# Feed-forward products: another order at the start of a block, wider h splits, residual updates spread

## The chip, the cores and the metric

One core of a Trainium2 chip runs the kernel. The metric is the device time of one execution in microseconds; three runs of the kernel before gave a median of 2126.9 (2126.14 to 2127.26).

## The reference, cut to what matters

The kernel computes one layer of a hybrid encoder for 512 rows of 2048 float32 values. A mixer (input projection, short convolution, gated linear attention) ends in an output projection with a residual. The change touches what comes behind it:

```python
    x = x + y @ w_out[l]
    h = rmsnorm(x, norm2_g[l])
    x = x + jnp.square(jax.nn.relu(h @ w_ff1[l])) @ w_ff2[l]
return rmsnorm(x, norm_f_g)
```

`w_ff1` is 2048 x 8192 and `w_ff2` 8192 x 2048. The change leaves what is computed as it is.

## The kernel before, in words

**Split products.** A float32 factor is held as two fp32r tiles: hi, a cast by ScalarE, and lo, the rest, subtracted by VectorE (`split_w`, lines 607 to 612, for weights). A product is three matmuls: hi by hi, hi by lo, lo by hi. So TensorE needs hi first, and lo two matmuls later at most.

**Seven products for eight.** Both feed-forward products are cut into 2 x 2 quarters, and seven products of sums of quarters (forms 1 to 7) replace eight. The weights' sums are w1 = b11 + b12 (form 5), w3 = w1 + b21 (form 6), w4 = w3 + b22 (form 4) and w7 = b11 + b21 (form 7), made by VectorE in `plus` (lines 614 to 617); forms 1, 3 and 2 are the raw quarters b12, b21, b22. Quarters come by SP's DMA queue into four raw buffers (`load_quarters`), and hi and lo have three buffers each, shared by all weights.

**The h forms.** While the output projection runs in column chunks 0 to 4 (`out_chunk`), `h_pair(p)` (lines 539 to 557) makes the forms of h for a pair of 128-column blocks: `h_block` transposes on TensorE and scales on VectorE, and `put_form` casts and subtracts one 128 x 256 form at a time. Pairs 0 to 6 are hooked into chunks 1, 2 and 4; pair 7 needs the last chunk and comes behind it, at line 580.

**First product, FF1** (lines 620 to 675). 32 steps g, each of seven products of 8 pairs x 3 = 24 matmuls of 128 x 256, in the order 1, 5, 7, 3, 6, 2, 4 (`product`). Results are combined, squared and, as forms for the second product, kept in DRAM (`a_keep`); the last two steps' results are kept whole in `a_last`.

**Second product, FF2** (lines 763 to 811). Four blocks of the inner dimension; in each, four column blocks n; in each n, two groups grp of seven products (`product2`), both in `ORDER` = 1, 6, 5, 3, 7, 2, 4. A product has 24 matmuls, in group 1 of the last block 12. `form(blk, grp, f)` (lines 689 to 706) brings one activation form from `a_keep` through a staging tile (four of them: two of tag st for even places in the order, two fixed slots of the h forms for odd places) and splits it; the first group's forms of the next block are made at n = 3 in group 1, the second group's at n = 0 in group 0. At the end of group 1, `evict` (lines 722 to 761) combines PSUM banks into four result tiles c, 128 x 512. In block 0 they are written to `c_keep`, in blocks 1 and 2 added to it by accumulating DMAs of the POOL queue, and in block 3 VectorE adds what `c_keep` holds (tile s, line 738) and updates the residual x with it (line 742, twice a tile).

**The end** (from line 837). The last 512 rows of `w_ff2` are multiplied in the plain way, tile e, and the final norm follows.

**What sets the order.** The program text gives every instruction a priority; when the kernel is built, a planner with times of its own puts each engine's instructions in a fixed order, the earliest of the text first among those that it holds ready. An instruction can so stand ahead of others that come earlier in the text. At run time each engine and queue takes its instructions in that fixed order and waits where one isn't ready.

Of the kernel before, what the change touches and what calls it, by code (L numbers as in the profile page):

```python
# [14 lines left out]
P = 128  # L15
# [24 lines left out]
def hymba_kernel(  # L40
# [444 lines left out]
    c_keep = [[tc.dram_tile([P, 2, HALF], F32, name=f"c_keep{n}{q}") for q in range(4)] for n in range(4)]  # L485
    hf = ctx.enter_context(tc.tile_pool(name="hf", bufs=1))
# [20 lines left out]
    def form_places(p):  # L507
        if p == 0:
            for n, f in enumerate(FORMS):
                wide_forms[f] = [  # L510
                    hf.tile([P, 4, HALF], F32R, name=f"S{q}{f}", tag=f"h{2 * n + m}") for m, q in enumerate("hl")
                ]
        if p < 4:
            for f in FORMS:
                hforms[p][f] = [t[:, p, :] for t in wide_forms[f]]
            return
        k = 2 * (p - 4)
        two = [
            [act.tile([P, 4, HALF], F32R, name=f"S{q}{p}{e}", tag=f"s{k + e + 8 * m}") for m, q in enumerate("hl")]
            for e in range(2)  # L520
        ]
        for n, f in enumerate(FORMS):
            hforms[p][f] = [t[:, n % 4, :] for t in two[n // 4]]

    def h_block(kt, pool):
        b = bank(f"htr_{kt}", "aux")
        n, k = divmod(kt, 4) if kt < 12 else divmod(kt - 6, 2)
        for i in range(NT):
            T.transpose(b[:, i * P : (i + 1) * P], xs[n][i][:, k * P : (k + 1) * P], ident)
        h = pool.tile([P, SEQ], F32, name=f"h_{kt}", tag=f"h{kt % 2}", bufs=1)  # L530
        V.scalar_tensor_tensor(out=h, in0=b, scalar=g2t[:, kt : kt + 1], in1=r1b, op0=ALU.mult, op1=ALU.mult)
        return h

    def put_form(p, f, src):
        hi, lo = hforms[p][f]
        S.copy(hi, src)
        V.tensor_tensor(out=lo, in0=src, in1=hi.bitcast(F32), op=ALU.subtract)

    def h_pair(p, pool):

        form_places(p)
        h1, h2 = (h_block(2 * p + e, pool) for e in range(2))
        a, b = slice(0, HALF), slice(HALF, SEQ)
        put_form(p, 1, h1[:, a])
        put_form(p, 2, h2[:, a])
        put_form(p, 4, h2[:, b])

        def minus(f, in0, in1):
            d = pool.tile([P, HALF], F32, name=f"d{f}_{p}", tag=f"d{f % 2}", bufs=2)
            V.tensor_tensor(out=d, in0=in0, in1=in1, op=ALU.subtract)  # L550
            put_form(p, f, d)
            return d

        d5 = minus(5, h1[:, b], h2[:, b])
        minus(7, h1[:, b], h1[:, a])
        d6 = minus(6, h1[:, a], d5)
        minus(3, h2[:, a], d6)

    with tc.tile_pool(name="n2", bufs=1) as n2:
# [36 lines left out]
    wt = ctx.enter_context(tc.tile_pool(name="wt", bufs=1, reuse_waits="tile"))  # L596

    def load_quarters(src, i0, n, name):

        raws = []  # L600
        for q in range(4):
            raw = wp.tile([P, UNIT], F32, name=f"raw_{name}{q}", tag="raw", bufs=RAWS)
            nc.sync.dma_start(raw[:, :n], src[i0 + q])
            raws.append(raw[:, :n])
        return raws

    def split_w(src, n, name):
        hi = wp.tile([P, UNIT], F32R, name=f"hi_{name}", tag="hi", bufs=3)
        lo = wp.tile([P, UNIT], F32R, name=f"lo_{name}", tag="lo", bufs=3)
        S.copy(hi[:, :n], src)  # L610
        V.tensor_tensor(out=lo[:, :n], in0=src, in1=hi[:, :n].bitcast(F32), op=ALU.subtract)  # L611
        return hi, lo

    def plus(in0, in1, n, name):
        w = wt.tile([P, 1024], F32, name=f"w_{name}", tag="w", bufs=3)
        V.tensor_tensor(out=w[:, :n], in0=in0, in1=in1, op=ALU.add)  # L616
        return w[:, :n]


    with tc.tile_pool(name="f1", bufs=1, reuse_waits="tile") as f1:  # L620
        for g in range(NPAIR):
            b12, b11, b21, b22 = load_quarters(w_ff1, 4 * g, 1024, f"f1_{g}")

            def product(f, w, dst, start):
                hi, lo = split_w(w, 1024, f"f1_{g}{f}")
                for p in range(8):
# [14 lines left out]
            product(1, b12, ba, True)  # L641
            q1 = half("q1")
            S.copy(q1, ba[:, :HALF])
            w1 = plus(b11, b12, 1024, f"f1_{g}5")
            product(5, w1, bc, True)
            q5 = half("q5")
            S.copy(q5, bc[:, :HALF])
            product(7, plus(b11, b21, 1024, f"f1_{g}7"), bd, True)
            product(3, b21, bc, False)
            w3 = plus(w1, b21, 1024, f"f1_{g}6")  # L650
            product(6, w3, bb, True)
# [35 lines left out]
    with tc.tile_pool(name="ff", bufs=1, reuse_waits="tile") as ff:  # L687
# [77 lines left out]
        for f in ORDER:  # L765
            form(0, 0, f)
        for blk in range(4):
            for n in range(4):
# [15 lines left out]
                for grp in range(2):  # L784
# [10 lines left out]
                    for f in ORDER:  # L795
# [10 lines left out]
                        if grp == 1:  # L806
                            evict(blk, n, f, dst, had)
# [154 lines left out]
```

## Time and profile before

| | us |
|---|---|
| median of 3 runs | 2126.9 |
| the profiled execution | 2126.53 |
| its span, first to last instruction | 2124.8 |
| TensorE busy | 2073.0 (98%) |
| VectorE busy | 1491.6 (70%) |
| ScalarE busy | 887.9 (42%) |
| POOL busy | 106.3 (5%) |
| FF1 begins / FF2 begins / last block of FF2 begins | about 786 / 1431 / 1916 |

The span lies inside the execution; 1.7 us lie around it. A matmul's listed duration (0.28 us) is longer than its share of the time, since matmuls overlap: what counts is the distance from one start to the next. The page's engines are PE (TensorE), PEld (its weight loads), DVE (VectorE), ACT (ScalarE), POOL (GpSimd) and SP (SyncE, a DMA queue here). A shape is partitions x elements.

### The profile page before, as it was taken

Reading aid. Unit: us, or ns where it says so; the run is one execution under the profiler, and the core shown is the slowest. Engines: PE = TensorE matmul, PEld = TensorE weight load, DVE = VectorE, ACT = ScalarE, POOL = GpSimd, SP = SyncE. Lnnn points to the kernel's source line nnn. Section 1 sums busy time; section 2 is a strip of 40 time slices with the busy share of each in tenths; the row PEclk is TensorE's granted clock in tenths of the full one; section 3 lists DMA queues with packets and bytes.
Section 4 is the critical chain, followed back from the end, with each engine's and each line's share of the span. In section 5 each row is a group of like instructions: output and inputs, shape, how many; then the busy total and the mean of one; then the engine's idle time right before and its main releaser. Section 6 shows DMA issues by size and latency. Waiting matters only on the chain.

```text
span 2124.8 us, 34341 instructions
## 1 busy us (share of the span) xinstructions
PE 2073.0 (98%) x14408; PEld 1925.0 (91%) x14408; DVE 1491.6 (70%) x1780; ACT 887.9 (42%) x1126; POOL 106.3 (5%) x161
## 2 busy tenths in 40 slices
PE   8999999999999999999999999999999999997987
PEld 7988878778788889999999999999999999997886
DVE  5232236756754468888888888888798798797786
ACT  6242213222233344554554554555354353353343
POOL 0000000000020000000000000000000001101000
PEclk9999999999999999999999999999999999999999
DMA  7223322222253324545445445457466476567342
GB/s 295 87 82 97 99 80 89 70 79 89 80 170 117 130 88 146 166 150 162 145 152 161 143 153 162 142 174 249 130 207 200 130 210 188 158 176 211 109 145 99
DMA packets 88314, 303.95 MB, mean 143 GB/s; under 512 B 10197, under 2 KB 10245, under 8 KB 87648
## 3 DMA queue, kind: packets, MB, share of 16 engines
q1 hardware_dynamic: 69120, 242.64, 35.9%
q0 software_dynamic: 19040, 59.13, 9.6%
q8 instruction: 112, 1.84, 0.4%
q14 instruction: 42, 0.34, 0.0%
HBM read 252.19 MB, written 49.55 MB: 142 GB/s over the span
## 4 chain that ended last, share of the span: by engine, by line
PE 91%; DVE 4%; DMA 2%; issue 1%; ACT 1%; ACTq 0%; DVEq 0%; POOLq 0%
PE f L717 23%; PE f1c L630 9%; PE f1a L630 8%; PE f1d L630 4%; PE f1e L630 4%; PE f1b L630 4%; PE tm_op L75 3%; PE tm_op L76 3%; PE tm_op L77 3%; PE fm_ch L75 2%; PE fm_cc L75 2%; PE tm_v L76 1%; PE tm_v L75 1%; PE tm_v L77 1%; PE fm_og L77 1%; PE fm_cb L76 1%
## 5 line engine op out<-in xcount | busy, mean ns | idle before, releaser
L717 PE MATMUL f<-lo_f,ah 128*128 128x256 f32 x1568 | 446.7, 285 | 20.2 <-DVE lo_f L611 20.2
L717 PE MATMUL f<-hi_f,ah 128*128 128x256 f32 x1568 | 443.3, 283 | 8.2 <-ACT ah L704 4.9
L717 PE MATMUL f<-hi_f,al 128*128 128x256 f32 x1568 | 443.9, 283 | 0.0
L610 ACT CAST hi_f<-w_f 128x1024 fp32r<-128x1024 f32 (+1 forms) x256 | 261.6, 1023 | 341.0 <-PE f L717 147.3
L611 DVE TENSOR_TENSOR lo_f<-w_f,hi_f 128x1024 fp32r<-128x1024 f32 (+1 forms) x256 | 303.9, 1189 | 120.6 <-ACT hi_f L610 119.3
L717 PEld LDWEIGHTS f<-lo_f,ah 128*128 128x128 f32 x1568 | 299.6, 191 | 21.9 <-DVE lo_f L611 21.8
L717 PEld LDWEIGHTS f<-hi_f,ah 128*128 128x128 f32 x1568 | 299.7, 191 | 8.6 <-ACT ah L704 5.1
L717 PEld LDWEIGHTS f<-hi_f,al 128*128 128x128 f32 x1568 | 300.0, 191 | 0.0
L610 ACT CAST hi_f<-raw_f 128x1024 fp32r<-128x1024 f32 (+1 forms) x192 | 196.5, 1024 | 198.1 <-PE f L717 82.9
L611 DVE TENSOR_TENSOR lo_f<-raw_f,hi_f 128x1024 fp32r<-128x1024 f32 (+1 forms) x192 | 227.4, 1184 | 3.6 <-ACT hi_f L610 3.6
L616 DVE TENSOR_TENSOR w_f<-raw_f,raw_f 128x1024 f32<-128x1024 f32 (+1 forms) x128 | 152.3, 1190 | 42.0 <-DMA raw_f<-in_w_ff 39.6
L616 DVE TENSOR_TENSOR w_f<-w_f,raw_f 128x1024 f32<-128x1024 f32 (+1 forms) x128 | 152.4, 1190 | 29.4 <-DMA raw_f<-in_w_ff 23.1
L630 PE MATMUL f1c<-Sh,hi_f 128*128 128x256 f32 x512 | 144.7, 283 | 3.2 <-ACT hi_f L610 3.2
L630 PE MATMUL f1c<-Sh,lo_f 128*128 128x256 f32 x512 | 144.7, 283 | 0.0
L630 PE MATMUL f1c<-Sl,hi_f 128*128 128x256 f32 x512 | 144.4, 282 | 0.0
L630 PE MATMUL f1a<-Sh,hi_f 128*128 128x256 f32 x512 | 144.2, 282 | 0.0
L630 PE MATMUL f1a<-Sh,lo_f 128*128 128x256 f32 x512 | 144.1, 282 | 0.0
L630 PE MATMUL f1a<-Sl,hi_f 128*128 128x256 f32 x512 | 144.0, 281 | 0.0
L75 PE MATMUL tm_op<-hi_op,yh 128*128 128x512 f32 (+1 forms) x304 | 106.2, 349 | 0.0
L76 PE MATMUL tm_op<-lo_op,yh 128*128 128x512 f32 (+1 forms) x304 | 105.3, 346 | 0.0
L77 PE MATMUL tm_op<-hi_op,yl 128*128 128x512 f32 (+1 forms) x304 | 105.0, 345 | 0.0
L630 PEld LDWEIGHTS f1c<-Sh,hi_f 128*128 128x128 f32 x512 | 97.4, 190 | 3.4 <-ACT hi_f L610 3.4
(359 smaller groups left out, 4846.3 us busy)
## 6 DMA issues: line engine op xcount, KB each, us to landing
raw_f<-in_w_ff SPq DMA_DIRECT2D x240, 512.0 KB, 3.8
a_keep<-y POOLq DMA_DIRECT2D x30, 896.0 KB, 5.1
st<-a_keep SPq DMA_DIRECT2D x49, 512.0 KB, 4.9
c_keep<-c POOLq DMA_DIRECT2D x48, 256.0 KB, 5.2
raw_op<-in_w_out SPq DMA_DIRECT2D x22, 512.0 KB, 3.6
raw_og<-in_w_feat SPq DMA_DIRECT2D x16, 512.0 KB, 3.6
raw_cc<-in_w_feat SPq DMA_DIRECT2D x16, 512.0 KB, 3.6
raw_ch<-in_w_feat SPq DMA_DIRECT2D x16, 512.0 KB, 3.7
```

The costliest lines, as they stand in the source:

```text
L75: T.matmul(dst, l[0], r[0], start=start, stop=False)
L76: T.matmul(dst, l[0], r[1], start=False, stop=False)
L77: T.matmul(dst, l[1], r[0], start=False, stop=stop)
L610: S.copy(hi[:, :n], src)
L611: V.tensor_tensor(out=lo[:, :n], in0=src, in1=hi[:, :n].bitcast(F32), op=ALU.subtract)
L616: V.tensor_tensor(out=w[:, :n], in0=in0, in1=in1, op=ALU.add)
L630: T.matmul(dst[:, :HALF], l[:, c], r, start=start and p == m == 0, stop=p == 7 and m == 2, skip_group_check=True,)
L717: T.matmul(d, l[:, k, t], r[:, c], start=grp == k == i == e == 0, stop=grp == 1 and k == m - 1 and e == 2, skip_group_check=True,)
```

## The change

- `load_quarters`, `split_w` and `plus` move up in the text; the pool `wt` is opened earlier, with two buffers for sums in place of three, and a pool `stage` takes over the two st tiles. `block_forms` makes a sum when its form is asked for, w3 and w4 in place of the sum that they start from.
- `h_pair` writes both transposed blocks into one tile of eight 256-wide places, makes the four differences in three operations, and from pair 4 on splits places 0 to 3 and 5 to 7 as two wide operations each.
- The first FF1 step: its weights are loaded ahead of `h_pair(7)` in the text, and forms 1, 5 and 7 are split there. Products 1, 5 and 7 run over pairs 0 to 6 first, and pair 7 follows.
- FF2: group 0 uses the order 1, 3, 2, 5, 7, 6, 4, group 1 the old one. `form` counts places by the group's own order; the loop that stages the second group's forms goes over group 0's order.
- Block 3: the rows of x come in 32 loads of 128 x 256, eight in each n behind group 0, where 8 loads of 128 x 1024 stood at n = 0. For n = 0 to 2 a result tile is added to s by an accumulating DMA of the POOL queue; for n = 3 VectorE adds it. The updates of x (`residual`) are put off: one tile's after each product of the next n's group 0, and those of n = 3 into the end, before the first update of columns 512 to 1023.

```diff
+    def block_forms(src, i0, n, name):
+        b12, b11, b21, b22 = load_quarters(src, i0, n, name)
+        w = {}
+        def parts_of(f):
+            if f in (5, 6) and 1 not in w:
+                w[1] = plus(b11, b12, n, f"{name}5")
+                w["early"] = f == 6
+            if f == 6:
+                w[3] = plus(w[1], b21, n, f"{name}6", None if w["early"] else w[1])
+            if f == 4:
+                w[4] = plus(w[3], b22, n, f"{name}4", w[3])
+            if f == 7:
+                w[7] = plus(b11, b21, n, f"{name}7")
+            v = {1: b12, 3: b21, 2: b22, 5: w.get(1), 6: w.get(3), 4: w.get(4), 7: w.get(7)}[f]
+            return split_w(v, n, f"{name}{f}")
+        return parts_of
...
+        V.tensor_tensor(
+            out=h[:, 0:2, :], in0=h[:, 4:5, :].to_broadcast([P, 2, HALF]), in1=h[:, 3:8:4, :], op=ALU.subtract
+        )
+        V.tensor_tensor(out=h[:, 5, :], in0=h[:, 3, :], in1=h[:, 1, :], op=ALU.subtract)
+        V.tensor_tensor(out=h[:, 2, :], in0=h[:, 6, :], in1=h[:, 5, :], op=ALU.subtract)
...
+        for e, (a, b) in enumerate(((0, 4), (5, 8))):
...
+            S.copy(hi[:, : b - a, :], h[:, a:b, :])
+            V.tensor_tensor(
+                out=lo[:, : b - a, :], in0=h[:, a:b, :], in1=hi[:, : b - a, :].bitcast(F32), op=ALU.subtract
+            )
...
+        first_forms = block_forms(w_ff1, 0, 1024, "f1_0")
+        ready = {f: first_forms(f) for f in (1, 5, 7)}
         h_pair(7, n2)
...
+            if g == 0:
+                for f, b in ((1, ba), (5, bc), (7, bd)):
+                    product(f, b, True, range(7))
+                product(5, bc, False, (7,))
+                product(1, ba, False, (7,))
+            else:
+                product(1, ba, True)
...
+                product(7, bd, False, (7,))
+            product(3, bc, False)
+            product(6, bb, True)
...
-    ORDER = (1, 6, 5, 3, 7, 2, 4)
+    ORDERS = ((1, 3, 2, 5, 7, 6, 4), (1, 6, 5, 3, 7, 2, 4))
...
+        def residual(n, q, c):
+            for i in range(2):
+                k = q // 2 * 2 + i
+                xc = x3t[k][q % 2][:, n, :]
+                V.scalar_tensor_tensor(
+                    out=xc, in0=c[:, i, :], scalar=r2[:, k : k + 1], in1=xc, op0=ALU.mult, op1=ALU.add
+                )
...
-                    V.tensor_tensor(out=t, in0=t, in1=had["s"][q], op=ALU.add)
...
+                    sq = had["s"][q]
+                    if n < 3:
+                        nc.gpsimd.dma_start(sq, t, accum_op=ALU.add)
+                    else:
+                        V.tensor_tensor(out=sq, in0=t, in1=sq, op=ALU.add)
+                    pending_sums.append(lambda: residual(n, q, sq))
...
+                    for f in ORDERS[grp]:
+                        product2(blk, grp, f, m, dst[f], *forms(f))
                         if grp == 1:
                             evict(blk, n, f, dst, had)
+                        elif pending_sums:
+                            pending_sums.pop(0)()
                         if (n, grp) == (0, 0):
                             form(blk, 1, f)
                         if (n, grp) == (3, 1) and blk < 3:
-                            form(blk + 1, 0, f)
+                            form(blk + 1, 0, ORDERS[0][ORDERS[1].index(f)])
+                    if (blk, grp) == (3, 0):
...
+                        for i in range(NT):
+                            for c in range(2):
+                                cols = slice(c * 1024 + n * HALF, c * 1024 + (n + 1) * HALF)
+                                nc.gpsimd.dma_start(x3t[i][c][:, n, :], x_keep[i][:, cols])
...
+                if i == 0 and n == 1:
+                    while pending_sums:
+                        pending_sums.pop(0)()
```

## Rows read from the trace of the kernel before

**Rows 1.** The page, part 4: chain that ended last, shares of the span by engine.

```profile
PE 91%; DVE 4%; DMA 2%; issue 1%; ACT 1%; ACTq 0%; DVEq 0%; POOLq 0%
```

**Rows 2.** Waits of TensorE: engine, line, waited for, us total, times, longest us.

```profile
PE f L717 <- DVE lo_f L611: 22.9, 12, 4.9
...
PE f L717 <- ACT ah L704: 4.9, 1, 4.9
...
PE f1c L630 <- ACT hi_f L610: 3.2, 1, 3.2
```

**Rows 3.** Chain in order of time, from 1425: start us, us, what.

```profile
1439.07 324.55 PE f L717 x2736
```

**Rows 4.** Windows: length, each engine's busy us (instructions), PEclk, DMA share, GB/s.

```profile
786.00:802.00 16.00, 11.06 (x79) 10.62 (x79) 15.53 (x31) 8.09 (x17) 0.88 (x2) 0.89 0.41 124
1431.00:1445.00 14.00, 9.14 (x65) 8.94 (x64) 12.48 (x12) 8.45 (x10) 0.55 (x1) 0.88 0.96 345
1757.00:1797.00 40.00, 37.72 (x315) 37.22 (x315) 32.89 (x32) 14.89 (x15) 1.73 (x2) 1.00 0.62 186
1916.00:1937.00 21.00, 16.15 (x119) 15.53 (x119) 11.30 (x13) 7.70 (x10) 3.37 (x5) 0.92 0.95 295
1937.00:1967.00 30.00, 23.24 (x177) 22.63 (x176) 25.44 (x38) 9.39 (x13) 2.17 (x4) 0.89 0.49 150
1967.00:2004.00 37.00, 31.99 (x252) 31.57 (x251) 29.68 (x41) 11.82 (x15) 2.15 (x4) 0.91 0.38 114
2004.00:2042.00 38.00, 32.94 (x259) 32.53 (x258) 30.21 (x43) 12.34 (x16) 2.15 (x4) 0.91 0.39 111
```

**Rows 5.** Timeline of VectorE, 785 to 798: start, us, line, operation, tiles, count.

```profile
786.40 1.41 DVE L531 SCALAR_TENSOR_TENSOR h<-htr,g2t,r1b 128x512 f32<-128x512 f32 x2 [0.42 <-PE htr L529]
...
790.15 1.21 DVE L616 TENSOR_TENSOR w_f<-raw_f,raw_f 128x1024 f32<-128x1024 f32 x1
...
793.92 1.19 DVE L611 TENSOR_TENSOR lo_f<-w_f,hi_f 128x1024 fp32r<-128x1024 f32 x1
```

**Rows 6.** Groups by line, VectorE, 700 to 794: count, busy us, mean ns, idle before.

```profile
L537 DVE TENSOR_TENSOR Sl<-d,Sh 128x256 fp32r<-128x256 f32 x24 | 9.5, 416 | 0.9 <-ACT Sh L536 0.9
...
L550 DVE TENSOR_TENSOR d<-h,d 128x256 f32<-128x256 f32 x12 | 5.0, 416 | 0.0
```

**Rows 7.** Timelines of the SP queue and of ScalarE, 1430 to 1460.

```profile
1431.41 4.97 SPq L698 DMA_DIRECT2D st<-a_keep  x4
...
1440.72 3.73 SPq L698 DMA_DIRECT2D st<-a_keep  x4
...
1450.33 3.73 SPq L698 DMA_DIRECT2D st<-a_keep  x3
...
1457.98 0.32 SPq L698 DMA_DIRECT2D st<-a_keep  x1
...
1437.97 4.10 ACT L704 CAST ah<-st 128x1024 fp32r<-128x1024 f32 x4
```

**Rows 8.** Timeline of the SP queue, 1925 to 1942.

```profile
1929.96 0.32 SPq L842 DMA_DIRECT2D st_e<-a_last  x1
```

**Rows 9.** Timeline of VectorE, 1951 to 1963.

```profile
1951.97 0.68 DVE L728 TENSOR_TENSOR c<-f,x 128x512 f32<-128x512 f32 x1
...
1957.56 1.66 DVE L742 SCALAR_TENSOR_TENSOR x<-c,r,x 128x256 f32<-128x256 f32 x4
...
1959.74 1.21 DVE L611 TENSOR_TENSOR lo_f<-raw_f,hi_f 128x1024 fp32r<-128x1024 f32 x1
```

**Rows 10.** Groups by line and shape, VectorE, 1940 to 2060.

```profile
L742 DVE SCALAR_TENSOR_TENSOR x<-c,r,x 128x256 f32<-128x256 f32 x24 | 10.2, 476 | 0.0
...
L738 DVE TENSOR_TENSOR c<-c,s 128x512 f32<-128x512 f32 x12 | 7.9, 681 | 0.0
```

**Rows 11.** Line 736: ns min/median/max of an issue; us to landing.

```profile
L736 POOL DMA_DIRECT2D c_keep<-c x32: 853/853/1231, 1630.8 to 1926.1; - x32
...
DMA to landing us min/median/max: 4.7/6.1/10.8
```

More of the change, by code (lines that the diff above doesn't have):

```diff
@@ L485, in hymba_kernel, with load_quarters, split_w, plus @@
     c_keep = [[tc.dram_tile([P, 2, HALF], F32, name=f"c_keep{n}{q}") for q in range(4)] for n in range(4)]
+    wt = ctx.enter_context(tc.tile_pool(name="wt", bufs=1, reuse_waits="tile"))
+    def load_quarters(src, i0, n, name):
+        raws = []
+        for q in range(4):
+            raw = wp.tile([P, UNIT], F32, name=f"raw_{name}{q}", tag="raw", bufs=RAWS)
+            nc.sync.dma_start(raw[:, :n], src[i0 + q])
+            raws.append(raw[:, :n])
+        return raws
+    def split_w(src, n, name):
+        hi = wp.tile([P, UNIT], F32R, name=f"hi_{name}", tag="hi", bufs=3)
+        lo = wp.tile([P, UNIT], F32R, name=f"lo_{name}", tag="lo", bufs=3)
+        S.copy(hi[:, :n], src)
+        V.tensor_tensor(out=lo[:, :n], in0=src, in1=hi[:, :n].bitcast(F32), op=ALU.subtract)
+        return hi, lo
+    def plus(in0, in1, n, name, into=None):
+        w = into
+        if w is None:
+            w = wt.tile([P, 1024], F32, name=f"w_{name}", tag="w", bufs=2)[:, :n]
+        V.tensor_tensor(out=w, in0=in0, in1=in1, op=ALU.add)
+        return w
+    def block_forms(src, i0, n, name):
[14 more added lines that the diff above has]
+        return parts_of
     hf = ctx.enter_context(tc.tile_pool(name="hf", bufs=1))
@@ L525, in h_block @@
[L525 to L557, printed above, removed]
+    PLACES = {7: 0, 5: 1, 3: 2, 1: 3, 6: 5, 2: 6, 4: 7}
@@ L594, in fbank, with product @@
         return fb.tile([P, 512], F32, name=name, tag="fb", bufs=8)
[L596 to L617, printed above, removed]
+    stage = ctx.enter_context(tc.tile_pool(name="stage", bufs=1, reuse_waits="tile"))
     with tc.tile_pool(name="f1", bufs=1, reuse_waits="tile") as f1:
         for g in range(NPAIR):
[L622 to L626, printed above, removed]
+            forms = block_forms(w_ff1, 4 * g, 1024, f"f1_{g}") if g else first_forms
+            def product(f, dst, start, pairs=range(8)):
+                if g or f not in ready:
+                    ready[f] = forms(f)
+                hi, lo = ready[f]
+                if 7 in pairs:
+                    del ready[f]
+                for p in pairs:
                     c = slice(p * P, (p + 1) * P)
@@ L657, in hymba_kernel @@
             V.tensor_tensor(out=y[:, 0, :], in0=q5, in1=v_, op=ALU.add)
-            product(2, b22, ba, False)
-            product(4, plus(w3, b22, 1024, f"f1_{g}4"), be, True)
+            product(2, ba, False)
+            product(4, be, True)
             S.activation(y[:, 2, :], ba[:, :HALF], AF.Relu)
@@ L737, in block @@
                 else:
[L738 to L744 removed]
+                    sq = had["s"][q]
+                    if n < 3:
+                        nc.gpsimd.dma_start(sq, t, accum_op=ALU.add)
+                    else:
+                        V.tensor_tensor(out=sq, in0=t, in1=sq, op=ALU.add)
+                    pending_sums.append(lambda: residual(n, q, sq))
             if f == 1:
@@ L764, in hymba_kernel @@
         x3t = None
-        for f in ORDER:
+        for f in ORDERS[0]:
             form(0, 0, f)
@@ L793, in hymba_kernel @@
[L793 to L805 removed]
+                    src, i0 = (
+                        (w_ff2, 4 * (8 * blk + 2 * n + grp)) if blk < 3
+                        else ((w_ff2, 4 * (24 + n)), (w_ff2_short, 4 * n))[grp]
+                    )
@@ L847, in hymba_kernel @@
             last_weights(n)
-        gft = [wt.tile([P, 4, HALF], F32, name=f"gft{c}", tag="st", bufs=2) for c in range(2)]
+        gft = [stage.tile([P, 4, HALF], F32, name=f"gft{c}", tag="st", bufs=2) for c in range(2)]
         for c in range(2):
```

113 lines of the change are left out of this document (47 added, 66 removed).

## The prediction

> **What bounds the kernel now.** I read the page's busy shares and its chain of waits first: TensorE carries 91% of the chain that ended last, over the whole span [rows 1]. So only two things can shorten the run: fewer matmuls, and the change removes none, or less time in which TensorE waits. The wait view says for whom it waits: nearly all of it is for the two halves of split operands, lo written by VectorE and hi or ah written by ScalarE, and all of that lies in the feed-forward part [rows 2]; between the first weights and the feed-forward part no wait is listed.
>
> How much is there to win? The chain in order of time gives TensorE's undisturbed pace: 2736 matmuls in 324.55 us, 0.1186 us each, so a product of 24 takes 2.85 us [rows 3]. A window is then read as its length less its matmuls times that pace [rows 4]: 6.6 us are lost where the first feed-forward product begins (16.00 less 79 x 0.1186), 6.3 where the second begins, 2.6 in its third block, 6.9 in the first group of its last block, 9.0, 7.1 and 7.3 in the three windows that each hold a step from one column block n to the next. Of the 9.0 I give the step 7.2, like the other two, and 1.8 to the group before. In all 45.8 us, 2.2% of the run, and nowhere else of such size. The granted clock column shows why a loss exceeds its wait: after each wait of about 5 us the mean is 0.88 to 0.91, so part of the window ran at 1.2 GHz in place of 2.4. At 1967 to 2004, 0.91 of 37 us means 3.3 us given away, while the window with a 2 us wait shows 1.00.
>
> **The change, part by part.** An estimate stands for each, with its bounds.
>
> *Start of the first product.* Now VectorE is the late one: the sum for form 5 begins at 790.15 and its lo half ends at 795.1, behind the h split of the last pair [rows 5]. The change makes forms 1, 5 and 7 of the weights before that pair and lets TensorE run 21 pair-products, 63 matmuls or 7.5 us, meanwhile, so the last pair is due 786.2 + 7.5 = 793.7. VectorE's work from 785.9, half a microsecond before its present start on that pair (786.40), until the pair is split: two sums and two lo halves at about 1.2 [rows 5], 4.8; two transposed scalings, 1.41 [rows 5]; a 512-wide and two 256-wide differences, 0.68 + 0.83; one 1024-wide lo, 1.2: 8.9 us, end 794.8, a wait of 1.2. Form 3 then needs a hi buffer, and all three were held: 1.03 cast [rows 7] plus 1.2 lo, less 0.6 of matmuls still to run, another 1.7. New loss 2.9 of 6.6, gain 3.7. Bounds: 5.4 if only the second wait is left and is short, 1.2 if both waits grow and the clock falls for some 3 us.
>
> *Wider sums and splits of h.* A pair now takes seven lo halves and four differences, 11 x 0.416 = 4.6 us [rows 6]. From pair 4 on it will be one 512-wide, two 256-wide, one 1024-wide and one 768-wide operation: 0.68 + 0.83 + 1.22 + 0.95 (between the neighbours) = 3.7. It saves 0.9 us a pair on VectorE; TensorE waits for none of it except the last pair, counted above. Nothing else to gain; if cover were gone, this would be a gain, not a loss.
>
> *Order of products and sums.* In a first group the order becomes 1, 3, 2, 5, 7, 6, 4, whose first three products take raw quarters, so no sum is due before the fourth. Sums stay four a group, so VectorE's total does not change; the sum buffers go from three to two, written in place. Counting by due times: a sum in place can follow as soon as the lo of the old content is done, and that is one to two products (2.9 to 5.7 us) ahead of its own cast in both orders. I price the lost buffer at nothing, hidden under those; if not hidden, 1.2 us per sum.
>
> What the new order does where FF2 begins is less good. The second form of the first group is still staged through a slot that the first product's h holds to the end: its four loads are issued from 1431.41, cast from 1437.97, and TensorE waits for that cast, whatever form it is [rows 2, 7]. And the forms of the second group are staged inside the loop over the first group's order, so form 6, used second there, is loaded sixth, behind form 2 in the same slot. That slot's cycles begin at 1431.4, 1440.7, 1450.3 and 1458.0 [rows 7]; form 6 moves from the third to the fourth. The shortest cycle shown is 7.7 us, so the fourth is ready about 1465.7. TensorE, which takes up FF2 at 1431.2, just before that slot comes free, comes there after eight products and its present loss: 1431.2 + 22.8 + 6.3 = 1460.3, 5.4 us before the form. I take 2.0 of that as lost, since TensorE's queue can hold another product of that group first. Loss 2.0; bounds +5 (raw form 2 runs in the wait) and -5 (a full wait, and the clock). In the third block I take 0 (+2.6, all of its loss gone, to -6, the same late form twice).
>
> *Last block, first group (8.7 lost).* DMA share is 0.95 [rows 4]. The x rows of 4 MB go from 8 loads to 32, placed later in the text. But their slots come free at the same moment as now, POOL is idle, and other loads are issued far ahead of their place in the text (the closing activations at 1929.96 [rows 8], some 130 us early), so I expect the same crowd; POOL pays 32 issues, at 0.85 each [rows 11] some 27 us in a block of 100, hidden. The sums moved off the start help a little: gain 1, bounds +7 and -5.
>
> *Steps between column blocks.* Here VectorE is the wait: before the first lo of the next n (1959.74) stand residual updates, four in a row from 1957.56 [rows 9]. A whole n has 12/3 = 4 additions at 0.68 and 24/3 = 8 updates at 0.476 [rows 10], 2.7 + 3.8 = 6.5 us, in a window of 37 us that has 29.9 us of TensorE's work. The change turns the four additions into accumulating DMAs and moves the updates behind the next products. Their new wait: a transfer of this kind lands 6.1 us after issue [rows 11]. The first c sum ends at 1952.65 [rows 9]; with 0.3 to issue it has landed at 1959.0, 2.9 after TensorE's end of this n (1956.1: that lo ends at 1960.95, and the wait for it was the longest, 4.9 [rows 2, 9]). If its update stands ahead of the second lo, that lo ends at 2.9 + 0.9 + 1.2 = 5.0 where 3.1 is due: a wait of 1.9, too short for the clock by these rows. So 7.2 becomes 1.9, three times: gain 15.9. Bounds: 21.6 with no wait; at worst all four updates stand ahead, the last landing 7.2 after, so 7.2 + 0.9 + 1.2 - 3.1 = 6.2 plus 3.3 of clock, 9.5 each, a loss of 6.9.
>
> The rows show POOL's issue of such a transfer at 853 ns at least and at the median of 32, beside a busy VectorE, so VectorE does not hold it up [rows 11]. The Trainium skill says otherwise, SBUF — State Buffer, section "SBUF: two separate sides": GpSimd cannot write descriptors while an operation of VectorE holds the port pair that they share, and a transfer of 620 ns took 3100. By that rule an estimate is 2.5 us more for each step, and the gain would be 8.4 in place of 15.9; this trace does not agree with it.
>
> *End.* The last n's updates leave VectorE's queue ahead of the closing products' splits. Four stand in a row there as at the steps, 4 x 0.476 = 1.9 [rows 10]; I take 1.7, bounds 3 and 0.
>
> Sum: 3.7 - 2.0 + 0 + 1.0 + 15.9 + 1.7 = 20.3. The profiled execution took 2126.5 (span 2124.8 and 1.7 around it), 0.4 under the median of 2126.9. So 2126.5 - 20.3 = 2106.2; for the median I say 2106.5.
>
> **The rivals.**
> *All waits go.* The planner puts updates behind the splits, the x loads spread, raw forms fill the wait at 1434: 5.4 + 5 + 2.6 + 7 + 21.6 + 2 = 43.6, 2083. For it: VectorE has the slack then (6.5 us of each n moved or gone). Against it: the staging slot.
> *A wait for accumulates takes the place.* The updates stand ahead and the step costs what it cost: the gain is 3.7 + 1.7 and little else, 2121. For it: VectorE takes its work in order. Against it: only the first landing comes after the step.
> *The issue of the accumulates is held up.* Each waits out the VectorE operation in progress, 1.2 at most [rows 5], three times 3.6: 2110. Against it: rows 11. (It is what the page's rule would do here.)
> *Slower: form 6 of the second group comes late in all four blocks.* One cycle of the slot is 9.3 us (1431.4 to 1440.7); its present margin is about 2.3 (split before the slot's next load at 1458.0, due 1460.3). A wait of 7.0 with some 1.7 of clock (0.11 of 16 us, as at 786 [rows 4]) is 8.7, four times 35; the other gains are 22.3, so 2126.5 + 12.7 = 2139. It decides as soon as that form lands later than 22.8 us after its block begins. Against it: in blocks two to four the second group's slots come free with the last products of the block before, so staging can begin earlier than at 1431.
> *The change does not do what it says*: the x loads are not spread. That is my own forecast for that term.
>
> **How the numbers follow.** Forecast 0.57, all waits go 0.15, accumulates take the place 0.14, issue held up 0.05, late form 0.09. Some 0.2%, 4.3 us, is what a measurement of this kernel can tell from no change. The accumulates' case, 5.4 us, straddles that: half of it counts as the same. With a tail of the forecast: faster 0.83, same 0.08, slower 0.09. The range leaves out about 1 in 10 at either end: 2089 (half of the way to the case without waits and more) to 2122 (the accumulates' case).
>
> **What would show it.** In the wait view, "DVE lo_f" falls from 22.9 to below 10 us, and the clock at 1967 to 2042 stays at 1.00. The windows after 786 and between the n steps lose about 3 and 2. A wait for ah or a of the second product of a second group shows the slot; VectorE idle before the residual line, released by a DMA on c, shows the accumulates. The prediction is wrong if the steps still lose over 5 us each, or if the DMA crowd of the last block grows past its 8.7.

## The result, and the profile after

The changed kernel takes 2111.4 us, the median of four runs (2106.2 to 2113.8), against 2127.1 before: a ratio of 0.9922, with an interval of 0.9900 to 0.9944. The forecast was 2106.5 (2089 to 2122): the sign and the range held, the gain is 15.7 in place of 20.4. The profiled execution took 2109.2, span 2107.5, 17.3 less than the span before.

The page, part 1, of the changed kernel, then its waits of TensorE (what waited, for whom, us in total, times, longest us):

```profile
PE 2070.4 (98%) x14408; PEld 1920.4 (91%) x14408; DVE 1489.1 (71%) x1740; ACT 885.2 (42%) x1106; POOL 130.3 (6%) x197
...
PE f L747 <- ACT hi_f L501: 5.6, 8, 0.9
PE f L747 <- DVE lo_f L502: 5.6, 11, 0.9
PE f L747 <- ACT ah L735: 5.3, 2, 4.6
PE htr L563 <- DVE xr L602: 3.5, 2, 3.2
PE f1c L653 <- ACT q L676: 0.9, 1, 0.9
```

The wait for lo fell from 22.9 [rows 2] to 5.6, and no wait on it is longer than 0.9. The longest one for ah, where FF2 begins, is 4.6 where it was 4.9 [rows 2]. A new one has come: the transposes of the last pair of h (htr) wait 3.2 us for the last residual addition of the output projection.

Windows of the changed kernel, columns as in [rows 4]: FF1's start, the first n of blocks 1 and 2, the last block's first group, and three stretches with one step between column blocks in each:

```profile
786.00:806.00 20.00, 15.79 (x114) 15.14 (x115) 16.29 (x27) 9.18 (x16) 1.20 (x3) 0.91 0.14 49
...
1597.00:1623.00 26.00, 23.73 (x191) 22.58 (x190) 22.18 (x20) 12.44 (x13) 1.05 (x2) 1.00 0.71 231
1760.00:1785.00 25.00, 22.36 (x181) 21.39 (x180) 21.70 (x20) 10.92 (x12) 1.08 (x2) 1.00 0.85 242
1922.00:1947.00 25.00, 22.66 (x172) 21.89 (x171) 17.41 (x20) 8.84 (x12) 12.92 (x23) 0.93 0.90 285
1947.00:1979.00 32.00, 30.89 (x259) 30.46 (x258) 27.70 (x38) 12.11 (x15) 5.74 (x8) 1.00 0.69 181
1979.00:2011.00 32.00, 30.93 (x259) 30.52 (x258) 27.28 (x37) 12.54 (x16) 5.72 (x8) 1.00 0.63 166
2011.00:2043.00 32.00, 30.76 (x255) 30.10 (x254) 29.55 (x39) 14.01 (x18) 6.77 (x10) 1.00 0.71 190
```

Read as the prediction reads them, length less matmuls times 0.1186: the steps lose 1.3, 1.3 and 1.8, at a clock of 1.00 (it was 0.89 to 0.91); FF1's start still loses 6.5; and block 1, where nothing was lost before, loses 3.4.

The table takes each stage from the start of its first matmul to the start of the next stage's, less its matmuls at 0.1186 (an undisturbed group of 168 reads -0.1). FF1's start runs from the projection's last matmul over the next 177.

| loss, us | before | after | gain | forecast |
|---|---|---|---|---|
| FF1's start | 6.9 | 7.1 | -0.2 | +3.7 |
| FF2's start (block 0, n = 0) | 6.4 | 7.6 | -1.1 | -2.0 |
| block 1, n = 0 | -0.2 | 3.6 | -3.9 | 0 |
| block 2, n = 0 | 2.8 | 3.8 | -1.0 | 0 |
| last block, first group | 9.1 | 4.8 | +4.2 | +1.0 |
| three steps | 22.2 | 5.2 | +17.0 | +15.9 |
| last group and closing products | 4.5 | 2.3 | +2.2 | +1.7 |
| sum | 51.8 | 34.4 | 17.4 | 20.3 |

So the last block gained more than forecast (23.4 against 18.6), and 6.2 us were lost ahead of it, where the forecast had a gain of 1.7.

### The profile page after: what moved, and what is told of

Its sections match the earlier page's. It is cut to its first block, busy times and chain, and to the rows that moved or that the text cites. A ratio compares the mean times of both kernels' runs of the same rounds, so it can differ in the third digit from the quotient of the medians.

```text
span 2107.5 us, 34328 instructions
## 1 busy us (share of the span) xinstructions
PE 2070.4 (98%) x14408; PEld 1920.4 (91%) x14408; DVE 1489.1 (71%) x1740; ACT 885.2 (42%) x1106; POOL 130.3 (6%) x197
## 5 line engine op out<-in xcount | busy, mean ns | idle before, releaser
L501 ACT CAST hi_f<-w_f 128x1024 fp32r<-128x1024 f32 (+1 forms) x256 | 261.8, 1024 | 337.0 <-PE f L747 113.9
```

## The experiments

Twelve kernels, each run beside the kernel before; a median is of four or five runs, for updates_at_once of eleven. First their times and losses, by the table's stages; block 1 and block 2 mean n = 0. The losses are of one profiled execution each. A stage that an edit leaves alone shows how far they scatter when the rest is planned anew: block 1 reads 3.3 to 4.7 in the runs that keep the new order there and two sum buffers, FF2's start 7.2 to 8.9. A difference of a microsecond in one stage so tells little.

| run | median | ratio, interval | FF1 | FF2 | block 1 | block 2 | first group | steps | end |
|---|---|---|---|---|---|---|---|---|---|
| changed kernel | 2111.4 | 0.9922, 0.9900 to 0.9944 | 7.1 | 7.6 | 3.6 | 3.8 | 4.8 | 5.2 | 2.3 |
| adds_on_vector | 2120.0 | 0.9959, 0.9945 to 0.9973 | 7.0 | 7.5 | 4.7 | 4.3 | 4.3 | 15.3 | 2.7 |
| updates_at_once | 2127.6 | 1.0004, 0.9995 to 1.0013 | 7.1 | 7.2 | 3.9 | 3.4 | 5.4 | 23.0 | 6.4 |
| order_old | 2110.8 | 0.9920, 0.9906 to 0.9933 | 6.7 | 5.3 | -0.2 | -0.2 | 6.9 | 18.0 | 2.0 |
| order_by_block | 2094.3 | 0.9844, 0.9829 to 0.9858 | 6.8 | 5.3 | -0.2 | -0.2 | 1.0 | 5.3 | 2.0 |
| sum_buffers | 2103.3 | 0.9886, 0.9873 to 0.9900 | 7.1 | 5.9 | -0.2 | 3.7 | 4.0 | 5.5 | 2.1 |
| ff1_start_old | 2110.0 | 0.9913, 0.9899 to 0.9926 | 6.5 | 8.1 | 4.0 | 3.9 | 5.1 | 5.8 | 2.3 |
| h_old | 2107.9 | 0.9904, 0.9889 to 0.9919 | 3.9 | 7.6 | 4.5 | 4.3 | 3.9 | 5.3 | 2.2 |
| x_loads_old | 2110.3 | 0.9917, 0.9902 to 0.9932 | 7.0 | 8.9 | 3.3 | 3.8 | 5.8 | 5.9 | 2.3 |
| ff2_stage | 2108.9 | 0.9910, 0.9894 to 0.9927 | 6.9 | 7.2 | 4.6 | 3.4 | 4.5 | 5.2 | 1.8 |
| block_and_h | 2094.5 | 0.9843, 0.9829 to 0.9856 | 5.4 | 5.9 | -0.2 | -0.2 | 1.7 | 5.3 | 2.1 |
| block_h_stage | 2094.8 | 0.9849, 0.9835 to 0.9862 | 5.6 | 7.8 | -0.2 | -0.2 | 0.3 | 6.5 | 1.4 |
| last_block_only | 2090.2 | 0.9823, 0.9809 to 0.9836 | 1.3 | 6.5 | -0.2 | -0.2 | 1.7 | 5.2 | 2.2 |

### What took the waits off the steps

**adds_on_vector**

```diff
-                    if n < 3:
-                        nc.gpsimd.dma_start(sq, t, accum_op=ALU.add)
-                    else:
-                        V.tensor_tensor(out=sq, in0=t, in1=sq, op=ALU.add)
+                    V.tensor_tensor(out=sq, in0=t, in1=sq, op=ALU.add)
```

> The changed kernel with the additions of the last block's results on VectorE again for every n (4 x 0.68 us each n), where it has accumulating DMAs for n = 0 to 2; updates stay put off. Theory (putting the eight updates of an n off its end is what removed the wait at the steps between n; the additions are not late): the three steps lose 0 to 1.5 more each, 2111 to 2116. Rival (the accumulating DMAs carry the gain, since VectorE has no room for additions and splits at a step): the steps lose 4 to 5.5 more each with the fall of the clock, 2123 to 2128.

Neither: the steps lose 10.1 us more, 3.1 to 3.8 each. Its VectorE timeline shows three additions ahead of the last lo of the old n (128x512) and the first of the next (128x1024):

```profile
1957.16 0.68 DVE L779 TENSOR_TENSOR s<-c,s 128x512 f32<-128x512 f32 x1
...
1958.95 1.28 DVE L779 TENSOR_TENSOR s<-c,s 128x512 f32<-128x512 f32 x2
1960.15 0.68 DVE L502 TENSOR_TENSOR lo_f<-w_f,hi_f 128x512 fp32r<-128x512 f32 x1
1960.76 1.22 DVE L502 TENSOR_TENSOR lo_f<-raw_f,hi_f 128x1024 fp32r<-128x1024 f32 x1
```

TensorE waits 2.0 us for the first of these two lo halves, behind a wait of 0.9 for a hi, and the window's clock is 0.95. So the accumulating DMAs are worth 3.4 of the 5.7 by which a step improved (7.4 to 1.7).

**updates_at_once**

```diff
-                    pending_sums.append(lambda: residual(n, q, sq))
+                    residual(n, q, sq)
```

> The changed kernel with the residual updates in their old place, right behind each result tile, while n = 0 to 2 keep the accumulating DMAs: each update then waits for a transfer that lands about 6 us after its issue. Theory (the rival of the prediction in which the accumulates take the place of the wait): the updates stand ahead of the next n's lo halves on VectorE, each of the three steps loses 5 to 9 with the fall of the clock, 2126 to 2136. Rival (the planner moves them behind the next splits of its own, so that putting them off in the text is not needed): 0 to 1 more each, 2111 to 2114.

The theory held: the steps lose 7.5, 7.7 and 7.7, as much as before the change. VectorE stands idle for the accumulates with the lo halves behind:

```profile
1958.67 0.88 DVE L756 SCALAR_TENSOR_TENSOR x<-s,r,x 128x256 f32<-128x256 f32 x2 [0.19 <-DMA s<-c]
1960.47 0.88 DVE L756 SCALAR_TENSOR_TENSOR x<-s,r,x 128x256 f32<-128x256 f32 x2 [0.92 <-DMA s<-c]
1962.65 0.88 DVE L756 SCALAR_TENSOR_TENSOR x<-s,r,x 128x256 f32<-128x256 f32 x2 [1.29 <-DMA s<-c]
...
1964.05 2.35 DVE L502 TENSOR_TENSOR lo_f<-raw_f,hi_f 128x1024 fp32r<-128x1024 f32 x2
```

This is the prediction's second rival, had the updates not been put off. They have to be put off in the text: the planner keeps them in front.

**order_old**

```diff
-    ORDERS = ((1, 3, 2, 5, 7, 6, 4), (1, 6, 5, 3, 7, 2, 4))
+    ORDERS = ((1, 6, 5, 3, 7, 2, 4), (1, 6, 5, 3, 7, 2, 4))
```

> The changed kernel with group 0 of FF2 in the old order 1, 6, 5, 3, 7, 2, 4; sums still in place with two buffers, all else stays. Theory (the new order bunches the four sums in products 4 to 7, while VectorE also splits the second group's forms, 1.2 + 1.2 + 1.2 us for a product of 2.85, so the n = 0 groups of blocks 1 and 2 lose 3.7 and 3.9 and the second group's form 6 comes 0.7 late where FF2 begins): block 1's first group loses under 0.5, the two blocks 2 to 3 together in place of 7.4 (less 2.4 that block 2 had before), FF2's start 1 less; 2105 to 2108. Rival one (the sums' two buffers cause it): those losses stay, 2110 to 2113. Rival two (the order is what took the last block's first group from 9.1 to 4.8): blocks 1 and 2 gain 5, the last block loses 4 again, 2109 to 2112.

Blocks 0 to 2 do what the theory says: 2.3, 3.9 and 4.0 us come back. The time does not: the steps lose 18.0 in place of 5.2 and the last block's first group 6.9 in place of 4.8. Windows of this run, block 1's first n and a step:

```profile
1594.00:1620.00 26.00, 26.00 (x223) 26.00 (x222) 24.71 (x22) 11.96 (x12) 0.54 (x1) 1.00 0.65 220
...
1940.00:1976.00 36.00, 31.67 (x239) 30.86 (x239) 27.04 (x37) 11.35 (x14) 5.72 (x8) 0.91 0.57 147
```

And VectorE at that step, then TensorE:

```profile
1951.86 1.22 DVE L509 TENSOR_TENSOR w_f<-w_f,raw_f 128x1024 f32<-128x1024 f32 x1
...
1955.09 0.48 DVE L756 SCALAR_TENSOR_TENSOR x<-s,r,x 128x256 f32<-128x256 f32 x1 [1.22 <-DMA s<-c]
1955.49 2.35 DVE L502 TENSOR_TENSOR lo_f<-w_f,hi_f 128x1024 fp32r<-128x1024 f32 x2
```

```profile
1948.87 0.39 PE L747 MATMUL f<-lo_f,a 128*128 128x256 f32 x1 [1.48 <-DVE lo_f L502]
...
1954.57 0.38 PE L747 MATMUL f<-hi_f,ah 128*128 128x256 f32 x1 [1.43 <-ACT hi_f L501]
...
1956.76 0.58 PE L747 MATMUL f<-lo_f,ah 128*128 128x256 f32 x1 [0.86 <-DVE lo_f L502]
```

The old order's second product is form 6, two sums deep. Its sum and an update that waits 1.22 for its DMA stand ahead of its lo. TensorE waits 1.48 for the last lo of the old n, and then, in the second product, for a hi and for that lo. So the new order does carry most of the gain at the steps, 12.8 of 17.0: it asks no sum of VectorE in the first three products. In blocks 0 to 2 it costs 10.2. By the medians the two cancel, 2110.8 against 2111.4, as the second rival said, though more of the loss is at the steps than in the first group; by the two profiled executions' losses the new order is 4 us ahead.

**order_by_block**

```diff
+    def places(blk, grp):
+        return ORDERS[grp if blk == 3 else 1]
...
-                    for f in ORDERS[grp]:
+                    for f in places(blk, grp):
```

> The changed kernel with the new order of group 0 in the last block alone; blocks 0 to 2 use the old order in both groups. Theory (the new order costs where a block begins, since four sums in a row meet the staging of the second group's forms, and gains at the steps of the last block, where it keeps sums off the first three products): the start of FF2 loses 5.3 in place of 7.5, blocks 1 and 2 nothing in place of 3.7 and 3.9, the three steps stay below 1 each; together 10 less, 2100 to 2103. Rival (the first block with the new order pays for it, so the crowd moves to the last block's beginning, or the planner's order of the last block depends on the blocks before): the last block loses 4 to 9 more, 2105 to 2110.

Better than the theory: 2094.3, 17 us under the changed kernel by the medians (15.4 by the profiled executions). Blocks 0 to 2 give 10 of them, as expected. The last block's first group, whose own order did not change, lost 1.0 in place of 4.8. The SP queue shows one difference: the last block begins at 1911.3 here and its last load of a form is issued at 1913.4; in the changed kernel it begins at 1922.6 and two such loads are still issued from 1927.6 on. The first row is of this run, the second, in its own fence, of the changed kernel:

```profile
1913.42 0.33 SPq L733 DMA_DIRECT2D st<-a_keep  x1
```

```profile
1927.63 4.61 SPq L729 DMA_DIRECT2D st<-a_keep  x2
```

Why the planner has the staging further along was not tried. From order_old this kernel differs in the last block's order alone. There the new order is worth 12.7 us at the steps and 5.9 in the first group, and 16.5 by the medians.

**sum_buffers**

```diff
-                w[3] = plus(w[1], b21, n, f"{name}6", None if w["early"] else w[1])
+                w[3] = plus(w[1], b21, n, f"{name}6")
...
-                w[4] = plus(w[3], b22, n, f"{name}4", w[3])
+                w[4] = plus(w[3], b22, n, f"{name}4")
...
-                w[7] = plus(b11, b21, n, f"{name}7")
+                w[7] = plus(b11, b21, n, f"{name}7", seventh[0](n, f"{name}7") if seventh else None)
```

(`seventh` holds a tile of the pool `stage`, tag w7, one buffer.)

> The changed kernel with a third sum buffer (form 7's sum has one of its own from the second FF1 step on) and no sum made in place of another, new order in all blocks. Theory (VectorE's work, not the buffers, is what the new order runs short of, four sums and four lo halves and four splits of forms in 11.4 us of TensorE): blocks 1 and 2 still lose 3 to 4.5 each, 2108.5 to 2112. Rival (the sums wait for a buffer, or for the lo half of the sum that they overwrite): those blocks lose under 1.5 each, 2104 to 2107.

Each theory has one block: block 1 loses nothing, block 2 as much as before. Windows of the two:

```profile
1595.00:1621.00 26.00, 26.00 (x222) 26.00 (x222) 24.31 (x22) 11.76 (x13) 0.97 (x2) 1.00 0.78 245
1754.00:1779.00 25.00, 23.15 (x181) 22.75 (x180) 21.52 (x20) 9.80 (x10) 1.18 (x2) 0.93 0.81 246
```

VectorE has the same work in either run. In the changed kernel's block 1 it goes without a pause from 1601.31 to 1616.15. The sum for form 4 takes the place of the one for form 6 there and comes behind that form's lo, 17.2 us after the block's first matmul (1597.70); with the third buffer it starts 11.4 us after it (1595.78). The first two rows are the changed kernel's, the row in the second fence this run's:

```profile
1612.66 1.22 DVE L502 TENSOR_TENSOR lo_f<-w_f,hi_f 128x1024 fp32r<-128x1024 f32 x1
...
1614.93 1.22 DVE L509 TENSOR_TENSOR w_f<-w_f,raw_f 128x1024 f32<-128x1024 f32 x1
```

```profile
1607.21 1.22 DVE L509 TENSOR_TENSOR w_f<-w_f,raw_f 128x1024 f32<-128x1024 f32 x1
```

What holds block 2 stays open. The whole is 8 us faster, by the medians.

### FF1's start

**ff1_start_old**

```diff
-        first_forms = block_forms(w_ff1, 0, 1024, "f1_0")
-        ready = {f: first_forms(f) for f in (1, 5, 7)}
         h_pair(7, n2)
...
-                for f, b in ((1, ba), (5, bc), (7, bd)):
-                    product(f, b, True, range(7))
-                product(5, bc, False, (7,))
-                product(1, ba, False, (7,))
+            product(1, ba, True)
```

> The changed kernel with its first FF1 step put back (weights loaded and split behind the last pair of h, products in the old order); all else stays. Changed kernel: 2111.4 median, and 7.1 us over TensorE's pace are lost from the last transposes to the end of that step's first products, against 6.9 in the kernel before. Theory (in the changed kernel VectorE does weight sums and wide h splits ahead of the last chunk's last residual addition, so the last pair's transposes come 3.2 us late and the clock falls; the new start only exchanges one wait for another): loss 6.5 to 7.5, time within 1.5 of the changed kernel, 2110 to 2113. Rival (the new start is worth the 3.7 that was predicted, and the loss seen is something that would be there in any case): loss 10 to 11, 2114.5 to 2116.

The number is the theory's, 6.5 lost and 2110.0. One part of its reason is not: the last pair still waits 3.15 for the addition, though the text now has the weights behind that pair. So the text's place of the weights does not decide that wait.

**h_old**

```diff
-    def h_pair(p, pool):
-        h = pool.tile([P, 8, HALF], F32, name=f"h_{p}", tag="h", bufs=1)
...
+    def h_pair(p, pool):
+        form_places(p)
+        h1, h2 = (h_block(2 * p + e, pool) for e in range(2))
```

(`form_places`, `h_block` and `put_form` of the kernel before come back with it.)

> The changed kernel with the h forms made as before (seven narrow lo halves of 0.42 us, four narrow differences); the first FF1 step stays new. Theory (the wide lo halves of pair 6, 0.95 and 1.22 us, stand with a weight sum of 1.22 ahead of the last chunk's last residual addition; narrow ones let it through, and then the new first step gains what it was meant to): the wait of 3.15 us before the last transposes goes, the loss at FF1's start falls from 7.1 to between 3 and 4.5, 2107 to 2109. Rival (the weight sums that the new first step puts early hold the addition up by themselves, or the narrow splits make the last pair later): loss 6 to 8, 2110 to 2112.5.

The theory held: 3.9 lost, and the wait for the addition is 0.24. In the changed kernel VectorE's timeline reads:

```profile
785.53 0.42 DVE L602 TENSOR_TENSOR xr<-tm_op,xr 128x256 f32<-128x256 f32 x1
...
786.20 1.22 DVE L509 TENSOR_TENSOR w_f<-w_f,raw_f 128x1024 f32<-128x1024 f32 x1
787.33 2.09 DVE L590 TENSOR_TENSOR Sl<-h,Sh 128x768 fp32r<-128x768 f32 x2
789.34 0.42 DVE L602 TENSOR_TENSOR xr<-tm_op,xr 128x256 f32<-128x256 f32 x1
```

The fourth of the last chunk's additions (line 602) follows the third by 3.8 us, behind a sum and pair 6's two wide lo halves. Then TensorE's clock falls, seen in the 0.91 of the window at 786.

**last_block_only** puts back the h forms, the first step and the order of blocks 0 to 2 (the diffs of h_old, ff1_start_old and order_by_block together). What it keeps of the change ahead of the last block is that the sums' pool wt opens ahead of the output projection, with two buffers and sums in place, and the pool `stage`.

> The kernel before with the last block's part of the change alone (new order of group 0 there, put-off updates, accumulating DMAs, x in 32 loads) and the two sum buffers; h, the first FF1 step and the order of blocks 0 to 2 are as before. Theory (the last block is all the gain; the new first FF1 step with narrow h splits gains 3): FF1's start loses 6.5 to 7 as before, 2093.5 to 2095.5, 3 more than with the new first step. Rival (the new first step is worth nothing once the h splits are narrow): 2090.5 to 2092.

Below both theories: 2090.2, the fastest of all, and FF1's start loses 1.3, with the old h splits and the old order of products. VectorE's timeline has the first two sums here:

```profile
760.07 1.23 DVE L509 TENSOR_TENSOR w_f<-raw_f,raw_f 128x1024 f32<-128x1024 f32 x1 [1.64 <-DMA raw_f<-in_w_ff]
...
766.30 1.23 DVE L509 TENSOR_TENSOR w_f<-raw_f,raw_f 128x1024 f32<-128x1024 f32 x1 [3.54 <-DMA raw_f<-in_w_ff]
```

They wait for their loads alone. In the kernel before, the first sum began at 790.15 [rows 5], 30 us later, behind the same text. What differs for a sum is where its pool opens: before, behind the closing of the pools of the residual rows (line 589 against 596), so that by the text its tiles stand in memory that the last pair still reads. That the pool is the cause is argued from these rows and the text; the pool was not moved alone, but fewer buffers and sums in place can't start a sum earlier.

**block_and_h** joins the diffs of order_by_block and h_old.

> Two edits together: the new order of group 0 in the last block alone, and the h forms as before; the first FF1 step, the two sum buffers and the spread updates stay as the change has them. Theory (the two are separate losses of the change, at FF1's start and in FF2, and add): 2094.3 less 3.2 to 3.5, 2090.5 to 2092, FF1's start loses 3.5 to 4.3. Rival (time won at FF1's start is lost again behind it, since the rest is planned anew): 2093.5 to 2095.

The rival: 2094.5, nothing gained. FF1's start loses 5.4, not 3.9. FF2's start and the last block's first group lose 1.3 more than in order_by_block, 0.6 and 0.7, which the scatter covers. The start's waits are the same as in h_old but for 0.06, and the clock is not: the first row is this run's window, the second h_old's.

```profile
785.00:805.00 20.00, 17.21 (x125) 16.15 (x124) 17.87 (x36) 9.80 (x22) 1.60 (x3) 0.91 0.26 80
```

```profile
786.00:806.00 20.00, 17.45 (x139) 16.61 (x140) 18.64 (x37) 10.56 (x23) 1.61 (x3) 1.00 0.26 80
```

From last_block_only this kernel differs in the new first step alone. So that step costs: FF1's start loses 5.4 with it and 1.3 without, and the medians are 2094.5 and 2090.2.

### Loads

**x_loads_old**

```diff
-                        for i in range(NT):
-                            for c in range(2):
-                                cols = slice(c * 1024 + n * HALF, c * 1024 + (n + 1) * HALF)
-                                nc.gpsimd.dma_start(x3t[i][c][:, n, :], x_keep[i][:, cols])
...
+                if (blk, n) == (3, 0):
+                    for i in range(NT):
+                        for c in range(2):
+                            nc.gpsimd.dma_start(
+                                x3t[i][c], x_keep[i][:, c * 1024 : (c + 1) * 1024].rearrange("p (a b) -> p a b", a=4)
+                            )
```

> The changed kernel with the rows of x in the last block loaded by 8 transfers of 128 x 1024 at n = 0, as before, in place of 32 of 128 x 256. Theory (the transfers were early and hidden either way; the last block's first group gained 4.2 from the order and the sums): that group loses 4.5 to 6.5 (4.8 in the changed kernel), 2110 to 2113. Rival (4 MB at the start of the last block are what crowded its weights and sums): it loses 8.5 to 10 again, 2114.5 to 2117.

The theory: the first group loses 5.8, 1.0 more than in the changed kernel, and the time is the same.

**ff2_stage**

```diff
-            if n % 2 and (blk, grp) != (3, 1):
-                raw = in_slot(second[14 + n // 2 % 2], name, F32)
+            late, k = (n % 4 > 1, n % 2) if (blk, grp) == (0, 0) else (n % 2, n // 2 % 2)
+            if late and (blk, grp) != (3, 1):
+                raw = in_slot(second[14 + k], name, F32)
```

> The changed kernel with the staging tiles of the first block's first group changed: forms one and two of the order through the st tiles, three and four through the two slots that the first product holds to its end (before and now: one and three through st, two and four through the slots). Theory (the wait of 4.6 us for the second form where FF2 begins is the slot's load, from 1431.4, and costs 6.5 with the clock): the second product waits under 1, the third form's load lands at 1436.2 and its cast ends at 1437.3, when it is due; loss 0.5 to 2.5 in place of 6.5, 2105.5 to 2108. Rival (the wait only moves to the third or fourth form, whose loads start at the same 1431.4): loss 4 to 6.5, 2109 to 2112.

The rival in kind: the 4.6 us wait is 1.2 now, and others came. TensorE's timeline of this run:

```profile
1438.82 0.39 PE L748 MATMUL f<-hi_f,ah 128*128 128x256 f32 x1 [1.20 <-ACT ah L736]
...
1450.43 0.39 PE L748 MATMUL f<-lo_f,ah 128*128 128x256 f32 x1 [1.67 <-DVE lo_f L502]
...
1455.12 0.39 PE L748 MATMUL f<-lo_f,ah 128*128 128x256 f32 x1 [0.87 <-DVE lo_f L502]
```

One reading, not tested alone, is that the slot's wait had given VectorE time to catch up and that without it the sums are late. FF2's start (with n = 0's second group) loses 7.2 in place of 7.6, no difference by the scatter.

**block_h_stage** joins ff2_stage's diff to block_and_h.

> As the run before it, and the second and third form of FF2's start exchange their staging tiles (two through st, three and four through the slots). In the changed kernel that left 6.2 of 6.5 lost, for the four sums in a row then came late. Theory (with the old order in block 0, sums are spread, so the wait at FF2's start really goes): that start loses 1 to 3 in place of 5.2, 2087 to 2089.5. Rival (VectorE can't make splits and sums of the first products faster in either order; the wait comes back in small pieces): 4.5 to 6, 2090 to 2092.5.

Neither theory: FF2's start loses 7.8, more than with the wait in it, and the time is the same as without the edit. The old order does not help there.

## Why the prediction was right, and where it was wrong

**Start of the first product, +3.7 forecast, -0.2 measured.** Two steps failed. "The change makes forms 1, 5 and 7 of the weights before that pair and lets TensorE run 21 pair-products": early sums are what counts as far as these rows show, and last_block_only has them (from 760.07) without the new order of pairs. It loses 1.3 with the old order, h_old 3.9 and block_and_h 5.4 with the new one (2.9 forecast for it). And "TensorE waits for none of it except the last pair", said of the wider h splits: the wide lo halves of pair 6 are ahead of an addition that the last pair needs. They cost 3.2 here (7.1 against 3.9), and 1.4 between order_by_block and block_and_h (6.8 against 5.4), where 0 was priced. The list of what is queued behind a moved instruction stopped at pair 7.

**FF2's start and the blocks, -2.0 forecast, -6.0 measured.** Form 6 of the second group came late by 0.7 only, and only in block 0, so the slot was rightly seen and mis-sized; no run had the "late in all four blocks" of the slower rival. The loss is in block 1, which the prediction did not cost, and the step that failed is "I price the lost buffer at nothing, hidden under those": with a third buffer and no sum in place block 1 loses nothing (3.6 of it), while block 2's loss stays. The buffer costs only together with the new order: with the old one and the same two buffers neither block loses anything (order_old, order_by_block). Sums stay four a group, as the prediction counts, but four in a row beside the splits of the second group's forms are not the same as four spread. Block 2 was priced at 0, with a bound of -6, and lost 1.0 more.

**Last block's first group, +1.0 forecast, +4.2 measured.** Mis-sized, inside the bounds. The term that was too small is "The sums moved off the start help a little: gain 1": between order_old and order_by_block the new order alone is worth 5.9 there, and order_by_block has 1.0 left. The x loads were not spread, as forecast: all 32 are issued between 1905.2 and 1938.5, and eight large ones in their place change nothing that can be told (2110.3).

**Steps, +15.9 forecast, +17.0 measured.** Right size, 1.9 forecast for each and 1.6, 1.6 and 2.0 left; the mechanism of what is left was wrong. The step "a transfer of this kind lands 6.1 us after issue" took a time into DRAM [rows 11] for one into SBUF. The rows of line 780 in the changed kernel (ns of an issue, who waited for it, us to landing):

```profile
L780 POOL DMA_DIRECT2D s<-c x12: 847/884/1172, 1955.6 to 2023.5; - x12
...
  DVE x L756: 1.1, 3
...
DMA to landing us min/median/max: 3.6/3.9/5.7
```

VectorE waits for them 1.1 us in all, one first update of 0.37 at each step. What TensorE waits for now is a hi, 0.90 at each of the three steps. By the order of the casts it is that of the next n's second product, form 3, whose first matmul stands in TensorE's fixed order ahead of the old n's last lo. ScalarE's cast of it waits until a product frees one of the three hi buffers, then takes 1.05 us. The changed kernel's VectorE, then its ScalarE, then TensorE:

```profile
1957.62 1.22 DVE L502 TENSOR_TENSOR lo_f<-raw_f,hi_f 128x1024 fp32r<-128x1024 f32 x1
1959.21 0.48 DVE L756 SCALAR_TENSOR_TENSOR x<-s,r,x 128x256 f32<-128x256 f32 x1 [0.37 <-DMA s<-c]
```

```profile
1954.66 1.06 ACT L501 CAST hi_f<-raw_f 128x1024 fp32r<-128x1024 f32 x1 [0.79 <-PE f L747]
1956.07 1.05 ACT L501 CAST hi_f<-raw_f 128x1024 fp32r<-128x1024 f32 x1 [0.36 <-PE f L747]
```

```profile
1957.17 0.38 PE L747 MATMUL f<-hi_f,ah 128*128 128x256 f32 x1 [0.90 <-ACT hi_f L501]
```

The first lo starts 1.90 after its own hi, the cast at 1954.66, is done, but it stands ahead of all updates; in the kernel before four updates stood ahead of it [rows 9]. The prediction gave the gain to the updates and the additions alone. The runs show three parts that are each needed: the new order (12.8), the put-off updates (17.8) and the accumulating DMAs (10.1). Each undone by itself gives back so much. The three don't add: their sum, 40.7, is far over 17.0, and without the put-off updates nothing of the gain at the steps is left.

The issue of these transfers was not held up: 847 to 1172 ns, each beside a running tensor_tensor of VectorE, so that rival is out. The Trainium skill, SBUF — State Buffer, section "Who interferes with whom", has VectorE's two-port modes take the whole pair of ports that the prediction weighed; of tensor_tensor it says, as an inference, that it takes the pair's read interface alone, while writing descriptors needs the write interface. These rows agree with that, and the prediction had drawn the rule too wide.

**End, +1.7 forecast, +2.2 measured.** Right. With the updates at once the end loses 6.4.

Why the total came near: the last block gave 4.8 us more than forecast, and the stages ahead of it fell 7.9 short of theirs. The two misses cancel in good part, so that the total came out near the forecast is in part luck.

## What to carry to other kernels

Take a change of several parts stage by stage: here one order of products was worth 12.8 us at the steps and cost 10 where a block begins, and using it in the last block alone made 2094.3 of 2111.4. Where the pool of a tile opens in the text can decide when its first write can start; an edit that looks like moving definitions is, by the argument above, what took FF1's start from 6.9 to 1.3. And before an operation is made wider, ask what small, urgent one stands behind it in its engine's queue.

## What was not expected of the hardware

An accumulating transfer of 256 KB landed in 3.9 us (median of 12) from SBUF into SBUF, against 6.1 (median of 32 [rows 11]) from SBUF into DRAM in the kernel before.

The clock falls on less than the prediction allowed. It called a wait of 1.9 "too short for the clock by these rows". In adds_on_vector waits of 0.9 and 2.0, 2.4 us apart, leave a window at 0.95; in block_and_h waits of 1.2 and 1.3, 1.8 us apart, were followed by a stretch at 1.2 GHz (0.91), and in h_old nearly the same two were not (1.00). A short wait so has two prices, 1.5 us apart at FF1's start (5.4 against 3.9), and these runs do not tell which one is paid.
